# A decoder block on one core: both parts of each plain weight chunk written by transfers from GpSimd's queue

## The chip, the core and the metric

The kernel runs on one core of a Trainium2 chip. A core has five engines that run side by side, each through its own instruction queue in order: TensorE (PE in the profile) multiplies matrices into PSUM, VectorE (DVE) and ScalarE (ACT) work elementwise on SBUF and PSUM, GpSimd (POOL) works elementwise on SBUF, and SyncE (SP) only issues transfers. Transfers between device memory (HBM) and SBUF run on 16 DMA engines; SP, ACT and GpSimd can issue them. Engines wait for one another by semaphores.

The metric is the device time of one execution in microseconds, lower is better.

## The reference, cut to what matters

The block computes, for 512 tokens of width 1024 in float32, a token mixer with three branches, a cross-attention into 256 memory tokens, and a squared-ReLU MLP with 4096 hidden columns:

```python
h = rmsnorm(x, norm_mix_g[l])
proj = h @ w_in[l]
cb, cc, ch, sq, sk, sv, rq, rk, rv, rg, gate_logits = jnp.split(proj, SPLIT_POINTS, axis=-1)
conv_out = short_conv_mixer(cb, cc, ch, conv_w[l], conv_b[l])
sb_out = stick_breaking_attention(sq, sk, sv)
ret_out = retention(rq, rk, rv, rg, ret_norm_g[l])
branches = jnp.stack([conv_out, sb_out, ret_out], axis=2)
up = jnp.einsum('bsnw,nwd->bsnd', branches, w_branch[l])
gates = jax.nn.sigmoid(gate_logits.reshape(b, s, N_BRANCH, D_MODEL) + b_gate[l])
merged = jnp.sum(gates * up, axis=2)
x = x + merged @ w_o[l]
h = rmsnorm(x, norm_xa_g[l])
mem_n = rmsnorm(mem, norm_mem_g[l])
x = x + memory_attention(h, mem_n, w_xq[l], w_xkv[l], w_xo[l])
h = rmsnorm(x, norm_mlp_g[l])
x = x + squared_relu_mlp(h, w_up[l], w_down[l])
return rmsnorm(x, final_g)
```

Nearly all the work is in products of an activation of 512 tokens (256 for the memory) with a weight matrix.

## The kernel before

**Two parts.** TensorE multiplies float32r, a rounded float32. To keep float32 accuracy each operand is written as a sum of a high part, the value rounded to float32r, and a low part, the value minus the high part, rounded again. A product is three matmuls: high by high, high by low, low by high (`mm3`, lines 234 to 236). Activations are split when they are made (`split`, lines 223 and 224), weights when they have been loaded.

**Chunks.** Every weight matrix lies in HBM in chunks of 128 partitions by 1024 float32 columns, 512 KB. There are two kinds of entries:

- `Plain` is one chunk. Its raw values come into a `w_raw` tile, and `parts_of` makes the parts: ACT writes the high part `wh` (line 111), VectorE the low part `wl` (line 112).
- `Seven` is two chunks for a product that is put together from seven smaller ones (`seven`, line 290). It has four steps: two make parts of raw halves and chunks, two make parts of mixtures that VectorE computes first (`w_mix`). It is used for half of the gates and for three quarters of the up projection.

**Buffers.** `w_raw` has 3 buffers (RAWS), `w_part` 11 (WBUFS). A plain chunk takes two `w_part` buffers, a Seven entry seven.

**The stream.** `run_plan` goes through the items of the plan in order. `Stream.loads` lists all raw loads in the order of first use and `Stream.steps` all steps; each step notes how many loads it needs. Before an item's matmuls `pump` makes the steps up to two beyond those the item needs (AHEAD), and ahead of each step `load` issues raw loads, up to three from the entry's first one, on SP's queue (line 178). The order in which each engine finally gets its instructions is not this program order: a scheduler goes through the whole program ahead of time and gives each engine the earliest instruction in program order that its own timing model holds to be ready and that has a free buffer. That order is then fixed.

**The start.** `first_loads` issues on SP the first tile of x, the gain, two raw chunks, the second tile of x, one more chunk, and the last two tiles of x. The first product (`sv`, the values of the stick-breaking attention) runs token tile by token tile, so that each of its four token tiles needs the same four chunks.

**What GpSimd does.** Constants at the start; two masks in each of the 32 stick-breaking steps (`diag`, line 479), one in front of VectorE's scan and one in front of TensorE's transpose; one product per rotary half (line 612) and per retention head (line 675); the power of -1/2 in every norm (line 348), which VectorE waits for. It issues no transfers.

Of the kernel before, what the change touches and what calls it, by code (L numbers as in the profile page):

```python
# [10 lines left out]
F32 = mybir.dt.float32  # L11
F32R = mybir.dt.float32r
AF = mybir.ActivationFunctionType
ALU = mybir.AluOpType

P = 128
# [11 lines left out]
CW = 1024  # L28
# [5 lines left out]
RAWS, WBUFS, AHEAD = 3, 11, 2  # L34
# [4 lines left out]
def trunk_kernel(ctx: ExitStack, tc: tile.TileContext, x, mem, par, rot, dqd, kdec, g_mix, g_xa, g_mem, g_mlp,  # L39
                 g_fin, w_in, w_gate, w_br, w_o, w_xq, w_xk, w_xv, w_xo, w_up, w_up7, w_down, out):  # L40
    nc = tc.nc
    te, act, dve, pool = nc.tensor, nc.scalar, nc.vector, nc.gpsimd

    const = ctx.enter_context(tc.tile_pool(name="const", bufs=1))
    wpool = ctx.enter_context(tc.tile_pool(name="wpool", bufs=1))
# [6 lines left out]
    def unit(name, shape=(P, 2, 512), dt=F32R):  # L52
        return upool.tile(list(shape), dt, name=name, tag="u", bufs=UNITS)
# [10 lines left out]
    class Split:  # L64


        def __init__(self, name, n, cols=512):
            self.per = 1024 // cols
            self.n, self.cols = n, cols
            self.h = [unit(name + "_h", (P, self.per, cols)) for _ in range(n // self.per)]  # L70
            self.l = [unit(name + "_l", (P, self.per, cols)) for _ in range(n // self.per)]
# [19 lines left out]
    def load_g(g, eng=None):  # L91
        g_bc = unit("g_bc", (P, D), F32)
        (eng or act).dma_start(out=g_bc, in_=g.rearrange("(o d) -> o d", o=1).broadcast_to([P, D]))
        return g_bc
# [8 lines left out]
    def parts_of(src):  # L103
        n = src.shape[1]
        part = lambda: wpool.tile([P, CW], F32R, name="w_part", bufs=WBUFS)
        if 2 * n <= CW:
            both = part()
            wh, wl = both[:, :n], both[:, n:2 * n]
        else:
            wh, wl = part(), part()  # L110
        act.copy(out=wh, in_=src)  # L111
        dve.tensor_tensor(out=wl, in0=src, in1=wh.bitcast(F32), op=ALU.subtract)  # L112
        return wh, wl

    class Plain:


        def __init__(self, t, c):
            self.loads = [(t, c)]
            self.steps = [lambda raw: parts_of(raw[0])]  # L120
            self.parts = []

        def get(self):
            return self.parts[0]
# [35 lines left out]
    class Stream:  # L160
        def __init__(self, entries):
            self.loads = [l for e in entries for l in e.loads]
            self.steps, first = [], 0
            for e in entries:
                e.first = first
                for i, st in enumerate(e.steps):
                    self.steps.append((e, st, first + (len(e.loads) if i else 1)))
                first += len(e.loads)
                e.last = len(self.steps)
            self.raw = {}  # L170
            self.nd = self.ns = 0
# [222 lines left out]
    def first_loads():  # L394
        xs = S["xs"] = [unit("x", (P, D), F32) for _ in range(NT)]
        ld = lambda t: nc.sync.dma_start(out=xs[t], in_=x[t * P:(t + 1) * P, :])
        st = S["stream"]
        ld(0)
        S["g"] = load_g(g_mix, nc.sync)
        act.preload_act_table_set("natural_log_exp_and_others")  # L400
        st.load(2)
        ld(1)
        st.load(3)
        ld(2)
        ld(3)
        act.dma_start(out=prm, in_=par)
        act.dma_start(out=kdt, in_=kdec)
        S["hT"] = Split("hT", KT)
# [4 lines left out]

    hT = lambda: S["hT"]
    item(first_loads)
    item(lambda: norm_x0(0))
    item(lambda: norm_T(0, S["hT"], 0))
# [733 lines left out]
```

## Time and profile before

| | us |
|---|---|
| median of 2 runs | 1033.89 (1033.83 to 1033.95) |
| the profiled execution | 1033.71 |
| its span, from the first to the last instruction | 1032.0 |
| TensorE busy in it | 1015.5 |
| VectorE busy | 648.8 |
| ACT busy | 500.7 |
| GpSimd busy | 66.2 |

The profile is one execution. A busy share is an average over stages with different limits; a row of a view names the line of the kernel, the engine, the operation, the tile written and the tiles read, a count after an x, the busy time and the mean of one in nanoseconds, and then the time that the engine sat idle in front of it with what ended it. Issue instructions of the transfers stand under SPq, ACTq and POOLq and are not counted as busy.

### The profile page before, as it was taken

The page shows a single profiled execution, that of the slowest core. Times are in us where ns is not written, and L with a number is a line of the kernel's source. Part 1 is how long each engine was busy: PE and PEld are TensorE (multiplying, and loading weights), DVE is VectorE, ACT ScalarE, POOL GpSimd, SP SyncE. Part 2 cuts the span into 40 slices and gives each one's busy share as a digit, 9 for nine tenths or more (in the row PEclk, how much of TensorE's full clock was granted, in tenths as well). Part 3 has the DMA queues.
Part 4 walks back from the last instruction along what each step waited for, and adds up shares of the span by engine and source line. Part 5 has one row for each costly group of instructions (what it writes and reads, how often), then busy time and mean ns, then how long its engine had stood idle before and what let it go on. Part 6 is the DMA issues. An engine that isn't in the chain of part 4 may idle for free.

```text
span 1032.0 us, 14325 instructions
## 1 busy us (share of the span) xinstructions
PE 1015.5 (98%) x5636; PEld 884.9 (86%) x5636; DVE 648.8 (63%) x992; ACT 500.7 (49%) x887; POOL 66.2 (6%) x118
## 2 busy tenths in 40 slices
PE   6999999999999999999999999999999999999997
PEld 4888888888888889998898888898889989989985
DVE  5567777856563796784584555466947566565643
ACT  6465567766532154463463444345416624643741
POOL 1101112321110000000100000000000000000000
PEclk9999999999999999999999999999999999999999
DMA  6322233213122212335354213223222321332222
GB/s 265 103 102 81 83 104 102 82 42 123 62 87 79 100 62 83 103 119 198 133 184 163 82 47 118 81 83 123 86 79 82 125 92 71 124 123 80 103 85 81
DMA packets 29876, 106.33 MB, mean 103 GB/s; under 512 B 3569, under 2 KB 3569, under 8 KB 29809
## 3 DMA queue, kind: packets, MB, share of 16 engines
q1 hardware_dynamic: 27216, 98.05, 27.7%
q10 hardware_dynamic: 2592, 7.37, 2.0%
q8 instruction: 44, 0.72, 0.3%
q14 instruction: 24, 0.19, 0.1%
HBM read 103.31 MB, written 2.10 MB: 102 GB/s over the span
## 4 chain that ended last, share of the span: by engine, by line
PE 97%; DMA 1%; DVE 0%; ACT 0%; SPq 0%; issue 0%; DVEq 0%; POOLq 0%; POOL 0%
PE mm L235 24%; PE mm L234 24%; PE mm L236 24%; PE p L290 17%; PE at L385 1%; PE o L546 1%; PE aT L512 1%; DMA w_raw<-in_w_in_dram 1%; PE z L488 1%; PE z L489 0%; PE xsc L236 0%; PE xsc L235 0%; PE xsc L234 0%; PE ro L693 0%; PE sc L667 0%; PE xpp L929 0%
## 5 line engine op out<-in xcount | busy, mean ns | idle before, releaser
L112 DVE TENSOR_TENSOR w_part<-w_raw,w_part 128x1024 fp32r<-128x1024 f32 (+1 forms) x180 | 210.9, 1176 | 168.1 <-PE mm L235 75.2
L111 ACT CAST w_part<-w_raw 128x1024 fp32r<-128x1024 f32 (+1 forms) x180 | 180.6, 1006 | 135.2 <-PE mm L236 79.1
L234 PE MATMUL mm<-hT_h,w_part 128*128 128x512 f32 (+1 forms) x512 | 193.6, 379 | 0.0
L235 PE MATMUL mm<-hT_l,w_part 128*128 128x512 f32 (+1 forms) x512 | 193.3, 378 | 0.0
L236 PE MATMUL mm<-hT_h,w_part 128*128 128x512 f32 (+1 forms) x512 | 193.0, 378 | 0.0
L290 PE MATMUL p<-mix_h,w_part 128*128 128x256 f32 x576 | 112.2, 283 | 0.5 <-ACT sv_s L297 0.5
L236 PEld LDWEIGHTS mm<-hT_h,w_part 128*128 128x128 f32 x512 | 96.4, 188 | 17.1
L234 PEld LDWEIGHTS mm<-hT_h,w_part 128*128 128x128 f32 x512 | 96.2, 188 | 16.8
L235 PEld LDWEIGHTS mm<-hT_l,w_part 128*128 128x128 f32 x512 | 96.5, 188 | 16.4
L235 PE MATMUL mm<-w_part,u_h 128*128 128x512 f32 x256 | 99.8, 390 | 0.0
L234 PE MATMUL mm<-w_part,u_h 128*128 128x512 f32 x256 | 98.6, 390 | 0.0
L236 PE MATMUL mm<-w_part,u_l 128*128 128x512 f32 x256 | 98.2, 389 | 0.0
L290 PEld LDWEIGHTS p<-mix_h,w_part 128*128 128x128 f32 x576 | 93.4, 192 | 1.4 <-ACT sv_s L297 0.7
L290 PE MATMUL p<-hT_h,w_part 128*128 128x256 f32 x432 | 84.4, 283 | 0.0
L290 PE MATMUL p<-mix_l,w_part 128*128 128x256 f32 x288 | 81.5, 283 | 0.0
L290 PEld LDWEIGHTS p<-hT_h,w_part 128*128 128x128 f32 x432 | 70.1, 192 | 0.8
L111 ACT CAST w_part<-w_mix 128x1024 fp32r<-128x1024 f32 x36 | 37.8, 1051 | 55.9 <-PE mm L235 37.5
L112 DVE TENSOR_TENSOR w_part<-w_mix,w_part 128x1024 fp32r<-128x1024 f32 x36 | 44.0, 1221 | 26.7 <-ACT w_part L111 20.0
L290 PE MATMUL p<-hT_l,w_part 128*128 128x256 f32 x216 | 60.7, 283 | 0.0
L236 PEld LDWEIGHTS mm<-w_part,u_l 128*128 128x128 f32 x256 | 48.1, 188 | 9.8
L235 PEld LDWEIGHTS mm<-w_part,u_h 128*128 128x128 f32 x256 | 48.1, 188 | 9.5
L234 PEld LDWEIGHTS mm<-w_part,u_h 128*128 128x128 f32 x256 | 47.9, 188 | 9.5
(211 smaller groups left out, 1813.2 us busy)
## 6 DMA issues: line engine op xcount, KB each, us to landing
w_raw<-in_w_in_dram SPq DMA_DIRECT2D x52, 512.0 KB, 3.4
w_raw<-in_w_up_dram SPq DMA_DIRECT2D x32, 512.0 KB, 3.6
w_raw<-in_w_down_dram SPq DMA_DIRECT2D x32, 512.0 KB, 3.4
w_raw<-in_w_br_dram SPq DMA_DIRECT2D x12, 512.0 KB, 3.4
w_raw<-in_w_gate_dram SPq DMA_DIRECT2D x12, 512.0 KB, 3.5
w_raw<-in_w_o_dram SPq DMA_DIRECT2D x8, 512.0 KB, 3.5
w_raw<-in_w_xk_dram SPq DMA_DIRECT2D x8, 512.0 KB, 4.2
w_raw<-in_w_xv_dram SPq DMA_DIRECT2D x8, 512.0 KB, 3.5
```

The source lines that it names most:

```text
L111: act.copy(out=wh, in_=src)
L112: dve.tensor_tensor(out=wl, in0=src, in1=wh.bitcast(F32), op=ALU.subtract)
L234: te.matmul(ps, lh, rh, start=first, stop=False)
L235: te.matmul(ps, lh, rl, start=False, stop=False)
L236: te.matmul(ps, ll, rh, start=False, stop=last)
L290: te.matmul(ps[:, :256], x[:, k, :], y, start=first and k == 0 and i == 0, stop=k == 3 and i == 2, skip_group_check=True)
L385: te.transpose(ps[:, k * P:(k + 1) * P], xn[:, c * P:(c + 1) * P], ident)
L488: te.matmul(z[:, :s], q[:, e, tsl], S["skh", hp][:, e, :s], start=True, stop=False)
L512: te.transpose(aps[:, sb * P:(sb + 1) * P], a[:, sb * P:(sb + 1) * P], ident)
L546: te.matmul(dst, vv, rhs, start=sb == 0 and i == 0, stop=sb == nblk and i == 1, skip_group_check=True)
```

## The change

For a plain chunk the raw load, ACT's rounding and VectorE's subtraction are replaced. The step now takes two `w_part` tiles, has GpSimd issue a transfer from HBM straight into `wh` that rounds to float32r on the way, has ACT write the negative of `wh` into `wl`, and has GpSimd issue a second transfer from the same HBM chunk that adds to `wl` in place. A plain entry lists no raw loads any more, so only Seven entries use `w_raw` and SP's queue, and the stream counts the loads that a step needs accordingly. The two calls that loaded raw chunks between the first tiles of x are removed.

```diff
         def __init__(self, t, c):
-            self.loads = [(t, c)]
-            self.steps = [lambda raw: parts_of(raw[0])]
+            self.loads, self.src = [], (t, c)
+            self.steps = [self.step]
             self.parts = []
+
+        def step(self, raw):
+            t, c = self.src
+            wh, wl = [wpool.tile([P, CW], F32R, name="w_part", bufs=WBUFS) for _ in range(2)]
+            pool.dma_start(out=wh, in_=t[c])
+            act.activation(out=wl, in_=wh.bitcast(F32), func=AF.Copy, scale=-1.0)
+            pool.dma_start(out=wl, in_=t[c], accum_op=ALU.add)
+            return wh, wl
...
                 for i, st in enumerate(e.steps):
-                    self.steps.append((e, st, first + (len(e.loads) if i else 1)))
+                    self.steps.append((e, st, first + (len(e.loads) if i else min(1, len(e.loads)))))
...
         ld(0)
         S["g"] = load_g(g_mix, nc.sync)
         act.preload_act_table_set("natural_log_exp_and_others")
-        st.load(2)
         ld(1)
-        st.load(3)
         ld(2)
         ld(3)
```

## The prediction

> **What bounds the kernel now.** I read the page's first lines and its table of engines, then the chain of work that ended last, then the busy time of each engine in stretches of the span, and only then the waits.
>
> ```profile
> span 1032.0 us, 14325 instructions
> PE 1015.5 (98%) x5636; PEld 884.9 (86%) x5636; DVE 648.8 (63%) x992; ACT 500.7 (49%) x887; POOL 66.2 (6%) x118
> ...
> PE 97%; DMA 1%; DVE 0%; ACT 0%; SPq 0%; issue 0%; DVEq 0%; POOLq 0%; POOL 0%
> ...
> 0.00:26.00 26.00, 16.76 (x63) 12.62 (x64) 14.47 (x26) 15.51 (x33) 2.96 (x12) 1.00 0.69 263
> 26.00:1010.00 984.00, 983.49 (x5509) 860.01 (x5508) 625.95 (x951) 482.68 (x847) 61.07 (x103) 1.00 0.29 99
> 56.00:237.00 181.00, 181.00 (x880) 151.32 (x879) 131.24 (x197) 114.61 (x218) 37.72 (x71) 1.00 0.24 82
> 447.00:590.00 143.00, 143.00 (x835) 126.68 (x834) 87.69 (x133) 69.04 (x123) 3.32 (x6) 1.00 0.43 149
> 1010.00:1032.00 22.00, 15.21 (x68) 12.25 (x66) 8.37 (x15) 2.54 (x8) 2.20 (x4) 0.95 0.25 95
> ```
>
> A row with a colon gives a stretch, then the busy time of PE, weight loads, DVE, ACT and POOL, the granted clock, the DMA share and GB/s. From 26 to 1010 us TensorE is busy for 983.49 of 984 us at full clock, so there the change can only lose. TensorE is free for 9.2 us in the first stretch and for 6.8 us in the last. The matmuls are untouched: even with both ends gone the span would be 1015.5 us. Work taken from VectorE buys almost nothing.
>
> **The change part by part: what goes.**
>
> ```profile
> L112 DVE TENSOR_TENSOR w_part<-w_raw,w_part 128x1024 fp32r<-128x1024 f32 (+1 forms) x180 | 210.9, 1176 | 168.1 <-PE mm L235 75.2
> L111 ACT CAST w_part<-w_raw 128x1024 fp32r<-128x1024 f32 (+1 forms) x180 | 180.6, 1006 | 135.2 <-PE mm L236 79.1
> ...
> L111 ACT CAST w_part<-w_mix 128x1024 fp32r<-128x1024 f32 x36 | 37.8, 1051 | 55.9 <-PE mm L235 37.5
> ...
> q1 hardware_dynamic: 27216, 98.05, 27.7%
> q10 hardware_dynamic: 2592, 7.37, 2.0%
> ...
> SPq L178 <- DVE w_part L112: 783.5, 143, 21.2
> ...
> DMA to landing us min/median/max: 3.3/3.5/8.3
> ```
>
> A Seven entry makes two parts from mixtures and two from loads. 36 mixture parts are 18 Seven entries, which take 36 of the 180 parts made from loads; 144 are plain chunks. For these, 144 subtractions leave VectorE, 144 x 1.18 = 170 us, worth 0 by the paragraph above: TensorE covers them. ACT keeps one pass per chunk: the negation is a pass of the size of the cast, so I take the cast's 1.05 us (bounds: the row's mean 1.01 and the mixture row's 1.05). Nothing is won or lost there.
>
> **What DMA gains in work.** SP's queue moved 98.05 MB in 27.7% of 1032 us, 286 us of all 16 engines; a 0.524 MB chunk is 1.53 us. The rounding transfer takes the place of the raw load; I take 1.53 us for it, since it moves the same bytes. The adding transfer is new. Its lower bound is a copy, 1.53 us; it must also fetch its own destination, which doubles what is read, so the upper bound that I use is 3.06 us, and I take that end because the second read has no way round. 144 x 3.06 = 441 us of DMA more in the whole kernel, on some 310 us: 73% of the span, enough on average, but not everywhere.
>
> The Trainium skill ("Collectives: The Full Stack", section "The bandwidth ceiling: the fold count and why AG ≠ RS ≠ AR") says that a reducing transfer ran at half a copy's rate because of its two source reads and not because of the addition. By that the sum is the one at 3.06; by the bare row of the copy, 1.53, the K/V term below would be nothing. No run here shows an adding transfer yet.
>
> **What latency grows.** SP's loads sit in three raw buffers and wait for VectorE to empty them (783.5 us of SP's time, 143 times); ACT and VectorE in turn wait for TensorE to give a w_part buffer back. So today a freed buffer is refilled in 1.05 + 1.18 = 2.2 us. After, a freed buffer must first be written by the rounding transfer, and a second one by ACT and the adding transfer: issue, landing 3.5, ACT 1.05, issue, landing 3.5 + 1.53. GpSimd's issue price stands in no row. The nearest are SP's issue and GpSimd's own longest kind of pass:
>
> ```profile
> L178 SPq DMA_DIRECT2D w_raw<-in_w_xk_dram x8: 327/328/328, 486.6 to 522.9; - x8
> ...
> 208.78 1.30 POOL L612 TENSOR_TENSOR r_sw<-r_sw,rot 128x512 f32<-128x512 f32 x1
> ...
> 20.25 0.39 PE L234 MATMUL mm<-w_part,hT_h 128*128 128x512 f32 x1
> ...
> 25.71 0.39 PE L234 MATMUL mm<-w_part,hT_h 128*128 128x512 f32 x1
> ...
> 523.21 0.28 PE L234 MATMUL mm<-mT_h,w_part 128*128 128x256 f32 x1
> ...
> 523.57 0.28 PE L234 MATMUL mm<-mT_h,w_part 128*128 128x256 f32 x1
> ...
> 380.50 7.19 PE p L290 x60
> ```
>
> I take 1.3 us, the GpSimd row, since the same engine does it in software; 0.33 is the low end. 288 issues are then 374 us, with the 66 us there 43% of GpSimd. A refill is 1.3 + 3.5 + 1.05 + 1.3 + 5.0 = 12.2 us. What covers it: 24 matmuls of 512 columns are one plain chunk, 25.71 - 20.25 = 5.46 us. Eleven buffers hold the chunk in use and 4.5 chunks behind it, 4.5 x 5.46 = 24.6 us. Covered. With 256 columns (w_xk) three matmuls take 0.36 us, a chunk 2.9 us, the cover 13 us: just enough, if DMA keeps up. A w_br chunk behind a Seven can start when the Seven before it has ended, one chunk and 84 matmuls of 0.12 us earlier, 5.46 + 10.1 = 15.5 us: covered by 3 us. So w_down, up7 and the gates cost 0; if a refill took 18 us instead, the six w_br chunks behind a Seven would cost 2.5 us each.
>
> **The start.** Two early loads leave SP's queue, so x comes earlier; but all four chunks of the first projection are needed for its first tokens, and the fourth chunk's low part decides now:
>
> ```profile
> 19.68 0.19 PEld L235 LDWEIGHTS mm<-w_part,hT_h 128*128 128x128 f32 x1 [0.28 <-DVE w_part L112]
> ```
>
> Before that point DMA must then bring one x tile and the gain row (3.1 us), four rounding transfers (6.1) and four adding ones (6.1 to 12.2): 15.3 to 21.4 us, from about 2 us on, with about 2 us to land. Beside them go three more x tiles, three raw chunks for the first Sevens, which are now asked for at the first pump instead of much later, and a fifth and sixth rounding transfer, 12 us at most. The low part comes between 19 and 36 us: 0 to +16, I take the middle, +8.
>
> **The K/V stretch.** From 447 to 590 us there are 32 plain chunks (w_o, w_xk, w_xv, w_xq, eight each). DMA is busy for 0.43 x 143 = 61 us. With 32 x 3.06 = 98 us more it is 159 us, 16 over the stretch; with 1.53 it is 110 and fits. Chunks held ahead take some of it: 0 to +16, I take +8.
>
> **GpSimd's queue.** It runs in order, and it holds the two masks of each of the 32 stick-breaking steps and the norms' powers. An adding transfer waits at its head for ACT's negation, and ACT for the landing: whatever stands behind it waits too, at most 3.5 + 1.05 us, and two issues of 1.3. Who waits then: VectorE's scan, ACT's exponential and TensorE's transposes. Their slack now:
>
> ```profile
> 69.75 0.29 POOL L479 TENSOR_SCALAR_AFFINE_SELECT sb_suf<-sb_suf 128x128 f32<-128x128 f32 x1 [2.85 <-ACT sb_suf L503]
> ...
> 73.94 0.27 PE L512 MATMUL aT<-ident,sb_suf 128*128 128x128 f32 x1
> 74.77 0.29 POOL L479 TENSOR_SCALAR_AFFINE_SELECT sb_suf<-sb_suf 128x128 f32<-128x128 f32 x1 [3.12 <-ACT sb_suf L503]
> ...
> 79.21 0.27 PE L512 MATMUL aT<-ident,sb_suf 128*128 128x128 f32 x1
> ```
>
> The mask ends at 70.04 and 75.06, the transpose starts 3.9 and 4.2 us later: about 4 us of slack. Two issues (2.6 us) fit in; a full block (7.15 us) overruns by 3.1 us, in all steps 32 x 3.1 = 100 us. The order is chosen ahead of time by readiness, so a transfer that is not ready should stand behind the next chunk's first transfer and the masks; I take a quarter of a microsecond per step, +8, between 0 and 100. The norms' powers wait in the same way, ten within the loop, 0 to 4.6 us each against a token's matmuls of 5.46 us: +2, and 0 if they fit. The last four come after the last transfer: 0.
>
> **Sum.** The profiled execution took 1033.7 us, against a median of 1033.9. 1033.7 + 8 + 8 + 8 + 2 = 1060 us.
>
> **The rivals.**
> - *All hidden but the start.* The buffers cover the refill, the second read is cheaper than a whole one, and masks stand ahead of the transfers. For it: 24.6 against 12.2 us, and the 4 us of slack. Against: the 0.43 DMA share of the K/V stretch. It decides when the adding transfer costs under about 2.5 us of all engines: then 61 + 32 x 2.5 = 141 us fits into 143. Time 1033.7 + 6 = 1040 us, not slower by 2%.
> - *The queue blocks in every step.* If GpSimd's order puts an adding transfer straight after its own rounding one, a chunk occupies the queue for 1.3 + 3.5 + 1.05 + 1.3 = 7.15 us, more than the 5.46 us of its matmuls. 1033.7 + 8 + 8 + 100 = 1150 us. Against it: an order by readiness, and eleven buffers that let four rounding transfers go first.
> - *The adding transfer is the bound.* It decides when both transfers take over 5.46 us, an addition over 3.9. At four copies, 6.1 us, the chunks take 144 x 7.65 = 1101 us of DMA; what else there is, (27.7 + 2.0)% of 1032 less 144 x 1.53, is 86: 1190 us or more. No row speaks for or against it.
> - *Faster.* Over 2% would be under 1013 us, below TensorE's 1015.5 us. It would take fewer matmuls.
>
> **How the numbers follow.** About 2% either way, 1013 to 1055 us, is what a measurement of this kernel can tell from no change. Forecast (some of each term, 1050 to 1080): 0.46. All hidden but the start: 0.33. Blocked queue: 0.11. Slow addition: 0.08. Faster: 0.02. So slower by over 2%: 0.46 + 0.11 + 0.08 = 0.65; within 2%: 0.33; faster: 0.02. The range goes from 1038 (the hidden case with a good start) to 1180 (the blocked queue with the upper ends at the start and in the K/V stretch), which leaves out the slow addition, the gain and the best of the hidden cases, some 0.17. The forecast's own range is 1050 to 1080.
>
> **What would show it.** VectorE at about 480 us, ACT still at 500; SP's queue down to some 22 MB and a new queue with 151 MB; HBM reads up by 75 MB. The first stretch should show TensorE waiting for an adding transfer at about 28 us; the 447 to 590 stretch should lengthen by about 8 us at a DMA share above 0.9; 700 to 1010 should keep its length. GpSimd's issues should be near 1.3 us, landings 3.5 and 5. Wrong would be: TensorE waits for w_part in the w_down stages (refill over 24 us, or DMA full), masks that come over 4 us late in most steps (the blocked queue), or no wait at all after 30 us.

## The result and the profile after

The changed kernel takes 1118.78 us (median of 2 runs, 1117.74 to 1119.83) against 1033.89 us. The ratio is 1.0821, 95% interval 1.0790 to 1.0852: slower by 85 us, where the prediction had +26 and a range up to 1180.

The page of the changed kernel: its span, the engines, three lines on DMA and the chain of work that ended last.

```profile
span 1118.1 us, 14424 instructions
...
PE 1043.2 (93%) x5636; PEld 894.8 (80%) x5636; DVE 486.1 (43%) x848; ACT 499.6 (45%) x887; POOL 263.0 (24%) x406
...
q0 software_dynamic: 41472, 151.01, 59.5%
q1 hardware_dynamic: 6480, 22.55, 5.6%
...
HBM read 178.81 MB, written 2.10 MB: 162 GB/s over the span
...
issue 22%; PE 17%; POOL 7%; DMA 5%; ACT 1%; DVE 1%; POOLq 0%; DVEq 0%; ACTq 0%
```

The work is what was foreseen: VectorE at 486 us, ACT at 500, 151 MB on the new queue, 22.55 MB on SP's. GpSimd's 263 us hold its issues of transfers: unlike SP's and ACT's, they stand under the engine itself here and count as busy. What is new is TensorE. Its idle time rose from 1032.0 - 1015.5 = 16.5 us to 1118.1 - 1043.2 = 74.9 us, and for the same 5636 matmuls it was busy 27.7 us longer. The chain, once 97% TensorE, now runs mostly elsewhere (its shares add up to about half of the span; the rest the view doesn't place, so I use it for this one statement only).

Where the time was lost: first or last matmul that reads a tile, from the views of the tiles, in us. The row of `z` is the first step of stick-breaking, `rt_out` the last up projection of the retention branch, `mgs` the product with w_o, `xq_h` the first scores of the cross-attention, `xo_h` the product with w_xo, `u_h` w_down.

| | z first | rt_out last | mgs last | xq_h first | xo_h first | u_h first | u_h last | span |
|---|---|---|---|---|---|---|---|---|
| before | 55.2 | 471.6 | 519.3 | 572.8 | 637.1 | 728.9 | 1024.4 | 1032.0 |
| after | 71.3 | 499.4 | 557.7 | 626.0 | 702.6 | 795.3 | 1108.0 | 1118.1 |
| later by | 16.1 | 27.8 | 38.4 | 53.2 | 65.5 | 66.4 | 83.6 | 86.1 |

The busy times of after in such stretches (PE, weight loads, DVE, ACT, POOL, clock, DMA share, GB/s):

```profile
0.00:56.00 56.00, 34.56 (x132) 26.94 (x133) 17.41 (x38) 19.93 (x46) 13.78 (x26) 0.94 0.67 190
60.00:270.00 210.00, 208.81 (x1010) 173.25 (x1009) 107.28 (x182) 129.69 (x242) 82.84 (x147) 1.00 0.79 174
499.40:626.00 126.60, 105.12 (x545) 87.10 (x544) 31.81 (x63) 43.41 (x82) 35.75 (x52) 0.95 0.88 221
...
795.30:1090.00 294.70, 282.47 (x1699) 250.87 (x1698) 140.28 (x206) 136.98 (x228) 40.07 (x56) 1.00 0.56 142
```

So there are three large places: the start (16.1 us), w_o to the cross-attention (rt_out last to xo_h first, 65.5 - 27.8 = 37.7 us, at a DMA share of 0.88 in its first part), and w_down (83.6 - 66.4 = 17.2 us, at a DMA share of only 0.56, a mean that is taken apart below). A smaller one, 27.8 - 16.1 = 11.7 us, lies between the first step of stick-breaking and the end of the up projections. The stick-breaking stretch, where the prediction feared GpSimd's queue, is not one: TensorE is busy 208.81 of 210 us (and waits another 2.05 us at 274.79, just behind the row).

Who waited for whom: TensorE's waits, then the longest of the other engines (sum, times, longest, in us).

```profile
PE at L393 <- DVE xn L384: 19.3, 3, 8.6
PE mm L243 <- DMA w_part<-in_w_down_dram: 7.0, 5, 2.8
PE mm L243 <- DMA w_part<-in_w_xv_dram: 5.9, 3, 2.8
PE mm L244 <- DMA w_part<-in_w_xk_dram: 5.4, 6, 1.6
```

```profile
POOL w_part L128 <- ACT w_part L127: 244.9, 103, 6.0
POOL w_part L126 <- PE mm L244: 172.0, 38, 22.9
POOL w_part L126 <- PE p L298: 161.8, 8, 52.4
...
ACT w_part L127 <- DMA w_part<-in_w_down_dram: 61.3, 22, 5.2
```

L126 is the rounding transfer, L127 the negation, L128 the adding transfer. The largest row is an adding transfer at the head of GpSimd's queue, held 103 times for ACT's negation, and ACT itself waits for the rounding to land (209 us in 77 places over all matrices). Roundings wait as well, 334 us in 46 places, for TensorE to give a buffer back; none of these waits falls between 566 and 642 us, the stretch shown next. The time from issue to landing, of line 126 and then of line 128:

```profile
DMA to landing us min/median/max: 3.6/6.3/11.9
```

```profile
DMA to landing us min/median/max: 5.2/6.9/12.3
```

The prediction had 3.5 and 5.0: these are the minima, not the medians. Last, GpSimd's own order in the stretch of w_xk, w_xv and w_xq (start, duration, line, idle time before it with its releaser):

```profile
566.04 0.88 POOL L128 DMA_DIRECT2D w_part<-in_w_xk_dram  x1 [2.78 <-ACT hT_h L231]
...
588.46 0.87 POOL L128 DMA_DIRECT2D w_part<-in_w_xv_dram  x1 [2.94 <-ACT w_part L127]
589.01 0.88 POOL L126 DMA_DIRECT2D w_part<-in_w_xv_dram  x1
592.52 0.87 POOL L128 DMA_DIRECT2D w_part<-in_w_xv_dram  x1 [2.63 <-ACT w_part L127]
593.07 0.88 POOL L126 DMA_DIRECT2D w_part<-in_w_xv_dram  x1
598.84 0.86 POOL L128 DMA_DIRECT2D w_part<-in_w_xv_dram  x1 [4.89 <-ACT w_part L127]
...
642.04 0.87 POOL L128 DMA_DIRECT2D w_part<-in_w_xq_dram  x1 [3.27 <-ACT w_part L127]
```

From 566 to 642 us the queue alternates strictly, adding, rounding, adding, rounding, and it always waits at the adding. Each adding belongs to the rounding before the last: the rounding of 589.01 gets its adding at 598.84, 9.8 us later, and in these 9.8 us two chunks go out. From 566.04 to 642.04 there are 16 intervals, 76.0 / 16 = 4.75 us per chunk. TensorE uses up a chunk of w_xk or w_xv in 2.9 us. The instruction list of GpSimd has this order nearly throughout: at 134 of the 144 addings exactly one further rounding stands in front, at the other 10 none.

### The profile page after: what moved, and what is told of

Its sections match the earlier page's. It is cut to its first block, busy times and chain, and to the rows that moved or that the text cites. A ratio compares the mean times of both kernels' runs of the same rounds, so it can differ in the third digit from the quotient of the medians.

```text
span 1118.1 us, 14424 instructions
## 1 busy us (share of the span) xinstructions
PE 1043.2 (93%) x5636; PEld 894.8 (80%) x5636; DVE 486.1 (43%) x848; ACT 499.6 (45%) x887; POOL 263.0 (24%) x406
## 3 DMA queue, kind: packets, MB, share of 16 engines
q0 software_dynamic: 41472, 151.01, 59.5%
q1 hardware_dynamic: 6480, 22.55, 5.6%
## 4 chain that ended last, share of the span: by engine, by line
issue 22%; PE 17%; POOL 7%; DMA 5%; ACT 1%; DVE 1%; POOLq 0%; DVEq 0%; ACTq 0%
PE p L298 5%; PE mm L243 4%; PE mm L244 4%; PE mm L242 4%; POOL w_part L126 4%; DMA w_part<-in_w_down_dram 3%; POOL w_part L128 3%; DMA w_part<-in_w_o_dram 2%; DMA w_part<-in_w_xo_dram 1%; ACT w_part L127 0%; DMA w_part<-in_w_up_dram 0%; DVE w_part L112 0%; DVE x L842 0%; PE at L393 0%; ACT w_part L111 0%
## 5 line engine op out<-in xcount | busy, mean ns | idle before, releaser
L127 ACT ACTIVATE w_part<-w_part 128x1024 fp32r<-128x1024 f32 x144 | 152.5, 1059 | 298.9 <-DMA w_part<-in_w_down_dram 61.3
L842 DVE TENSOR_TENSOR x<-mm,x 128x512 f32<-128x512 f32 x48 | 32.4, 688 | 72.4 <-PE mm L244 72.4
L126 POOL DMA_DIRECT2D w_part<-in_w_down_dram x32 | 25.4, 795 | 157.0 <-PE p L298 155.7
L128 POOL DMA_DIRECT2D w_part<-in_w_in_dram x52 | 45.7, 878 | 59.2 <-ACT w_part L127 38.0
```

The source lines that it names most:

```text
L126: pool.dma_start(out=wh, in_=t[c])
L127: act.activation(out=wl, in_=wh.bitcast(F32), func=AF.Copy, scale=-1.0)
L128: pool.dma_start(out=wl, in_=t[c], accum_op=ALU.add)
L842: dve.tensor_tensor(out=dst, in0=ps, in1=dst, op=ALU.add)
```

## The experiments

**What a transfer costs by itself.** Nothing but transfers of 512 KB chunks: eight of each kind in a row, then one of each alone. The kernel leaves the whole block out.

```diff
+        ("pool_round", F32R, lambda t, s: pool.dma_start(out=t, in_=s)),
+        ("pool_add", F32, lambda t, s: pool.dma_start(out=t, in_=s, accum_op=ALU.add)),
```

> Only transfers of 512 KB chunks, in groups of eight: loads from SP, plain loads from GpSimd, rounding ones, adding ones without and with rounding; then one of each alone. Theory A (the second read of the adding transfer is the price): eight loads and eight rounding ones take 12 to 14 us of all engines, eight adding ones 24 to 26; alone an adding one lands 1.5 us after a rounding one. Theory B (the transfers are cheap, the fixed order of the queues is the price): all groups take 12 to 14 us, and an adding one alone lands in under 4 us.

Median us to landing, of eight and of one:

```profile
sp_copy<-in_w_in_dram SPq DMA_DIRECT2D x8, 512.0 KB, 7.1
...
pool_round<-in_w_in_dram POOLq DMA_DIRECT2D x8, 512.0 KB, 7.1
pool_add<-in_w_in_dram POOLq DMA_DIRECT2D x8, 512.0 KB, 11.7
...
pool_round_one<-in_w_in_dram POOLq DMA_DIRECT2D x1, 512.0 KB, 3.7
pool_add_one<-in_w_in_dram POOLq DMA_DIRECT2D x1, 512.0 KB, 5.1
```

Its timeline shows the pace of a full queue, since VectorE reads one value of each chunk as soon as it lands:

```profile
50.34 0.15 DVE L59 COPY tok<-pool_round 128x1 f32<-128x1 f32 x1 [1.12 <-DMA pool_round<-in_w_in_dram]
51.61 0.15 DVE L59 COPY tok<-pool_round 128x1 f32<-128x1 f32 x1 [1.12 <-DMA pool_round<-in_w_in_dram]
...
74.26 0.15 DVE L59 COPY tok<-pool_add 128x1 f32<-128x1 f32 x1 [2.35 <-DMA pool_add<-in_w_in_dram]
76.77 0.15 DVE L59 COPY tok<-pool_add 128x1 f32<-128x1 f32 x1 [2.35 <-DMA pool_add<-in_w_in_dram]
```

A rounding transfer lands every 51.61 - 50.34 = 1.27 us, as a copy from SP does (1.28); an adding one every 76.77 - 74.26 = 2.51 us. Rounding is free, adding costs twice a copy, and the upper end that the prediction took was right in kind. That the fetch of the destination is what doubles the time, and not the addition, no run here separates; "the second read" below stands for both. Alone they land after 3.7 and 5.1 us, as predicted. The Trainium skill's sentence that the prediction cited ("Collectives: The Full Stack", section "The bandwidth ceiling: the fold count and why AG ≠ RS ≠ AR"), half a copy's rate for a reducing transfer, agrees with this run. Both transfers of a chunk together need 3.78 us of a full queue, more than the 2.9 us of a chunk of 256 columns.

**The second read taken away.** The second transfer overwrites instead of adding, so the low part is the chunk rounded once more and not the remainder; the order of GpSimd's queue stays the same.

```diff
-            pool.dma_start(out=wl, in_=t[c], accum_op=ALU.add)
+            pool.dma_start(out=wl, in_=t[c])
```

> The adding transfer is replaced by a second rounding one, so the low part holds the high part; order of all queues and every wait as in the changed kernel. Theory A (DMA work and landing time of the adding transfer): at least half of the 85 us comes back, 1075 us or less, the K/V stretch and the w_down rounds nearly as before. Theory B (GpSimd's and ACT's queues wait in order for the rounding transfer's landing): the waits are all still there, 1100 us or more.

1057.30 us (1055.79 to 1058.64), ratio 1.0227 (1.0211 to 1.0242): 61.5 of the 85 us are gone.

```profile
q0 software_dynamic: 41472, 151.01, 44.1%
```

The same bytes take 44.1% of 1054.1 us instead of 59.5% of 1118.1 us, 200 us less, 1.4 us per adding. A rounding transfer now lands after 4.6 us (median) instead of 6.3.

**The negation on VectorE instead of ACT.**

```diff
-            act.activation(out=wl, in_=wh.bitcast(F32), func=AF.Copy, scale=-1.0)
+            dve.tensor_scalar(out=wl, in0=wh.bitcast(F32), scalar1=-1.0, scalar2=None, op0=ALU.mult)
```

> VectorE writes the negative instead of ACT. Theory B with ACT as the blocked queue (210 us of ACT waiting for rounding transfers, norms and splits behind it): 20 us or more come back, under 1100 us. Theory A: ACT's wait only fills time in which DMA is late anyway, within 10 us of 1119.

1123.89 us, ratio 1.0873 (1.0855 to 1.0891): no gain. The wait for the landing costs no less in VectorE's queue than in ACT's; what it costs in either, this run does not tell. In the changed kernel's own timeline it shows twice: the sums of squares of the third token tile stand in ACT's queue behind negations that waited 6.39 and 2.77 us for landings, and start at 37.73 us instead of 22.28, and TensorE's wait of 2.05 us at 274.79 is for an exponential of stick-breaking behind a negation that waited 4.88 us.

**One stage the old way.** For the named chunks the raw load, ACT's rounding and VectorE's subtraction are put back: the four chunks of the first product; those of w_o, w_xk, w_xv and w_xq; those of w_down.

```diff
+            if 'w_in' in t.tensor.name and 20 <= c < 24:
+                self.loads = [(t, c)]
+                self.steps = [lambda raw: parts_of(raw[0])]
```

> Only the four chunks of the first projection are made the old way (load on SP, ACT rounds, VectorE subtracts). If the loss of 23 us at the start comes from these chunks' chain of transfers, 15 to 23 us come back: 1096 to 1104. If it comes from what stands behind in GpSimd's queue (norm powers behind later chunks' transfers), less than 10 come back.

> The 32 chunks of w_o, w_xk, w_xv and w_xq are made the old way, all others by transfers. If the K/V stretch loses its 37 us to its own transfers (DMA work of rounding and adding there), 30 us or more come back: 1080 to 1090. If the delay is only carried in from earlier (late norms, late start), less than 15 come back.

> The 32 chunks of w_down are made the old way. Refill theory (after a Seven entry only four buffers are left, and a refill of some 16 us is longer than the 11 us of cover): the 17 us of the four rounds come back, 1098 to 1104. If the rounds are late because of DMA work carried over from before, less than 8 come back.

| old way for | us | ratio (interval) | less than after |
|---|---|---|---|
| first product | 1114.50 | 1.0766 (1.0743 to 1.0789) | 4 |
| w_o, w_xk, w_xv, w_xq | 1081.71 | 1.0462 (1.0443 to 1.0481) | 37 |
| w_down | 1099.91 | 1.0634 (1.0586 to 1.0682) | 19 |

The last two agree with the table of places. The first does not: with it `z` begins at 63.4 us, 8 earlier than after, but `xo_h` at 701.2, only 1.4 earlier. What was won at the start was lost again where the parts run short.

**One half of the change alone.** First the adding half: SP loads raw, ACT rounds and negates, GpSimd only adds. The transfers' work stays the same. Then the rounding half: GpSimd rounds, SP loads raw too, VectorE subtracts.

```diff
-            pool.dma_start(out=wh, in_=t[c])
+            act.copy(out=wh, in_=raw[0])
```

> SP loads the raw chunk ahead as before, ACT rounds it into the high part and writes its negative, GpSimd's transfer adds: the same DMA work as in the changed kernel (a copy and an addition per chunk), but the first half of the chain is hidden behind the raw buffers. DMA-work theory: little changes, 1095 to 1120. Chain theory (issue, landing, negation, issue, landing in a row): at least 30 us come back, under 1090.

```diff
-            act.activation(out=wl, in_=wh.bitcast(F32), func=AF.Copy, scale=-1.0)
-            pool.dma_start(out=wl, in_=t[c], accum_op=ALU.add)
+            dve.tensor_tensor(out=wl, in0=raw[0], in1=wh.bitcast(F32), op=ALU.subtract)
```

> GpSimd's transfer rounds into the high part, SP loads the raw chunk, VectorE subtracts: two copies per chunk in DMA and no addition. DMA-work theory: as with the copy in place of the addition or better, 1040 to 1058. Chain theory: the same wait for a landing from GpSimd's queue stands in front of VectorE, 1060 or more.

The adding half takes 1083.67 us, ratio 1.0481 (1.0466 to 1.0497): with the same bytes and the same 144 addings 35 us are gone, so the DMA engines' throughput alone is not the cause. The rounding half takes 1044.99 us, ratio 1.0110 (1.0095 to 1.0125); its `z` begins at 64.0 us, 8.8 late, and that is nearly all of its 11 us.

**More and fewer buffers.** My theory at this point was the prediction's own picture with larger numbers: a refill of 0.87 + 6.3 + 1.06 + 0.87 + 6.9 = 16 us against what the buffers hold.

```diff
-UNITS, SCRS = 30, 9
-RAWS, WBUFS, AHEAD = 3, 11, 2
+UNITS, SCRS = 28, 9
+RAWS, WBUFS, AHEAD = 3, 13, 2
```

> The changed kernel with 13 w_part buffers instead of 11 (and two activation buffers fewer, to make room). Theory A (a freed buffer's refill, 0.87 + 6.3 + 1.06 + 0.87 + 6.9 = 16 us at the median, outlasts what the other buffers hold): one chunk more ahead gives 5.5 us more cover at 512 columns and 2.9 at 256, so at least 20 us come back, 1099 us or less, with the K/V and w_down stages shorter. Theory B (the DMA engines' throughput alone): the same bytes and the same doubled reads in the same stretches, within 8 us of 1118.8.

> The kernel before with the same 13 w_part buffers and two activation buffers fewer: the control for the run with 13 buffers. Both theories: its refill is 2.2 us, covered by far, and TensorE is busy without a gap, so within 3 us of 1033.7. If the activation buffers matter, it is slower, and that difference is to be taken off the other.

With 9 buffers UNITS stays at 30.

> The changed kernel with 9 w_part buffers, all else the same. Theory A: 3.5 chunks held behind the one in use cover 19 us at 512 columns and 10 at 256, against a refill of 16 at the median and up to 25: at least 30 us more than the change, 1149 us or over. Theory B (DMA throughput): within 8 us of 1118.8.

> The kernel before with 9 w_part buffers, the control: both theories, within 5 us of 1033.7, since 2.2 us of refill are covered by 3.5 chunks as well as by 4.5.

| w_part buffers | after | before |
|---|---|---|
| 9 | 1120.87, ratio 1.0840 (1.0809 to 1.0871) | 1033.98, 1.0002 (0.9993 to 1.0011) |
| 11 | 1118.78, ratio 1.0821 (1.0790 to 1.0852) | 1033.76 |
| 13 | 1125.85, ratio 1.0887 (1.0855 to 1.0919) | 1036.72, 1.0031 (1.0019 to 1.0042) |

The theory fell: neither 20 us won nor 30 lost. But DMA throughput, its rival, had already fallen by the adding half alone. A third is needed, and the order of GpSimd's queue gave it: with 13 buffers as well, exactly one rounding stands in front of 134 addings. More buffers cannot be used by an order that never asks for them.

**Three roundings ahead.** A chunk's step first issues the roundings of the next two plain chunks. `round` issues a chunk's rounding if it hasn't been issued. At 123 of the 144 addings (121 with 13 buffers) three roundings now stand in front. The second kernel has the overwriting transfer (its low part is not the remainder), the third 13 buffers.

```diff
+            for _ in range(3):
+                if isinstance(e, Plain):
+                    e.round()
+                    e = e.next
```

> The changed kernel, but a chunk's step first issues the roundings of the next two plain chunks (unless a Seven entry stands between), so that GpSimd's queue holds three roundings ahead of each adding transfer instead of one; same transfers, same buffers, same engines. Theory C (the in-order queue with one rounding ahead sets a period of half a rounding's landing, negation and issues, 4.6 us per chunk in the K/V stretch): the period falls to what the DMA engines allow, 3.8 us (1.27 + 2.5), the K/V stretch gives back some 15 of its 37 us and w_down most of its 19: 1075 to 1095 us. Theory B (the DMA engines' throughput): within 8 us of 1118.8.

> The same three roundings ahead, with a plain transfer in place of the adding one (the low part is then the raw chunk, not the remainder). Theory C with the DMA engines as the second bound: without the second read a chunk takes 2.5 us of DMA, less than the 2.9 of the K/V stretch, and with the deeper queue nothing is left but the start: 1040 to 1050 us, 10 us or so below the 1057 of the copy with one rounding ahead. If the queue is not it: 1057 again.

> The three roundings ahead with 13 w_part buffers (two activation buffers fewer, worth +3 us in the kernel before). Theory C: if the buffers bind once the order allows them, 5 us or more below the run with 11; if the DMA engines bind by then, within 5 us of it.

| | us | ratio (interval) |
|---|---|---|
| three ahead, 11 buffers | 1110.48 | 1.0735 (1.0712 to 1.0759) |
| three ahead, 11 buffers, overwriting | 1058.83 | 1.0252 (1.0228 to 1.0275) |
| three ahead, 13 buffers | 1084.05 | 1.0494 (1.0477 to 1.0510) |

The order alone gives 8 us and misses its expectation; the buffers alone gave nothing; both together give 35. The waits with 11 buffers say why (L128 is the rounding here, L139 the adding):

```profile
POOL w_part L128 <- PE mm L257: 307.1, 75, 23.0
...
POOL w_part L139 <- ACT w_part L138: 99.4, 85, 6.0
```

Addings wait 99 us instead of 245, but the roundings in front of them now wait 307 us for TensorE to free a buffer, and hold up the addings behind. With 13 buffers the queue runs like this at w_xq:

```profile
583.10 0.88 POOL L139 DMA_DIRECT2D w_part<-in_w_xq_dram  x1 [2.01 <-ACT w_part L138]
...
586.78 0.88 POOL L139 DMA_DIRECT2D w_part<-in_w_xq_dram  x1 [2.25 <-ACT w_part L138]
...
594.30 0.87 POOL L139 DMA_DIRECT2D w_part<-in_w_xq_dram  x1 [2.29 <-ACT w_part L138]
```

594.30 - 583.10 is three intervals, 3.73 us per chunk: the 1.27 + 2.51 us of the transfers measured by themselves. Here the DMA engines are the bound: from 560 to 600 us they move 282 GB/s at a share of 1.09 (the share adds up the packets' times and can pass 1). The changed kernel had 222 GB/s at a share of 0.95 from 566 to 642 us, so a share near 1 was not yet the ceiling there. Without the second read, three ahead is worth nothing (1058.83 against 1057.30 with one ahead), which misses too. As far as these runs show, one rounding ahead is too few only while the adding transfers make the roundings land late.

**What is left.** All three have three roundings ahead and 13 buffers. The first moves the power of -1/2 of the norms of one token tile to ACT; the second has the first four chunks and the first loads as before; the third has this start and overwrites instead of adding.

```diff
-        pool.tensor_tensor(out=r, in0=ms, in1=half[:, :n], op=ALU.pow)
+        if n == 1:
+            act.activation(out=r, in_=ms, func=AF.Ln)
+            act.activation(out=r, in_=r, func=AF.Exp, scale=-0.5)
```

> Three roundings ahead, 13 buffers, and the power of -1/2 of the norms of one token tile made by ACT (a logarithm and an exponential on 128 values) instead of GpSimd. If the start is late because the powers stand behind adding transfers in GpSimd's queue: the first stick-breaking step 8 us or more earlier than without, and 1076 us or less. If it is late because the first chunks' low parts land late: within 4 us of 1084.

> Three roundings ahead, 13 buffers, and the four chunks of the first product made the old way, with the two early raw loads put back between the tiles of x. Theory (the start's delay is the four chunks on GpSimd's queue, and it was given back later only because the supply of parts bound there): the first stick-breaking step some 12 us earlier than without, and most of it kept to the end: 1068 to 1075 us. If it is given back again: 1080 or more.

> As the run with three roundings ahead, 13 buffers and the old start, with a plain transfer in place of the adding one (the low part is then the raw chunk, not the remainder). Theory (start, queue order, buffers and the second read are all there is): as the kernel before with 13 buffers, 1036.7, to within 5 us. If something else costs time (GpSimd's issues in front of the masks, the powers, the clock), 1045 or more.

The powers on ACT take 1096.25 us, ratio 1.0608 (1.0589 to 1.0627), 12 more than without, and `z` begins at 73.2 us instead of 70.9: neither expectation. They brought in table loads, 13 on each of the two new lines:

```profile
L370 ACT ACT_TABLE_LOAD x13 | 16.7, 1283 | 0.2
L371 ACT ACT_TABLE_LOAD x13 | 16.7, 1283 | 0.2
```

That is 33 us more on the engine that makes the negations. The changed kernel's own timeline answers the question that this run does not: each of its 22 powers starts at most 0.72 us after the value that it reads is made, so none stood behind a transfer for long.

With the old start the kernel takes 1071.72 us, ratio 1.0369 (1.0352 to 1.0385), as expected: `z` begins 13.8 us earlier (57.1 against 70.9), and 12.3 us remain at the end. With the supply of parts loosened, a gain at the start is kept.

The last takes 1040.67 us, ratio 1.0066 (1.0051 to 1.0082), 4 us above the kernel before with 13 buffers. Its page, then GpSimd's queue at w_xq (L131 is the rounding):

```profile
span 1038.6 us, 14440 instructions
...
PE 1018.4 (98%) x5636; PEld 884.4 (85%) x5636; DVE 489.0 (47%) x852; ACT 500.5 (48%) x887; POOL 206.7 (20%) x398
```

```profile
542.03 0.53 POOL L131 DMA_DIRECT2D w_part<-in_w_xq_dram  x1 [1.33 <-PE mm L260]
...
544.91 0.53 POOL L131 DMA_DIRECT2D w_part<-in_w_xq_dram  x1 [1.33 <-PE mm L260]
```

One chunk every 544.91 - 542.03 = 2.88 us, and the queue waits for TensorE: the supply is ahead again. The whole loss is now laid out, in this order of removal: order and buffers 1118.78 to 1084.05, 34.7 us; the start, to 1071.72, 12.3; the second read, to 1040.67, 31.1; a rest of 4.0 to the kernel before with 13 buffers, and the 3.0 that this kernel itself takes more than with 11. Unrounded that is 85.0, the difference to 1033.76. The sizes hang on the order of removal: the second read taken away first is worth 61.5, and then the queue's order is worth nothing. The lengths of the stages, from the views of the tiles, show which step repaired which:

| us | before | after | three ahead, 13 buffers | and old start | and overwriting |
|---|---|---|---|---|---|
| to z first | 55.2 | 71.3 | 70.9 | 57.1 | 57.2 |
| z first to rt_out last | 416.4 | 428.1 | 417.5 | 420.7 | 416.3 |
| rt_out last to xo_h first | 165.5 | 203.2 | 183.1 | 184.7 | 165.3 |
| xo_h first to u_h first | 91.8 | 92.7 | 92.5 | 92.4 | 91.9 |
| u_h first to last | 295.5 | 312.7 | 308.1 | 307.2 | 298.3 |

Order and buffers repair the second row and half of the third; the second read is the other half of the third, and the larger part of w_down's. Two other runs agree on w_down: 295.4 us with its chunks made the old way, and 297.6 with the overwriting transfer and one rounding ahead.

Why w_down feels the transfers at a DMA share of 0.56 is told in part by the changed kernel's timeline. That share is a mean of rounds of eight chunks of w_down and of the Seven products between the rounds (columns as above):

```profile
872.00:911.00 39.00, 35.88 (x195) 30.63 (x193) 8.72 (x16) 18.29 (x29) 11.30 (x16) 1.00 0.89 216
911.00:960.00 49.00, 48.78 (x333) 45.41 (x334) 33.09 (x47) 22.89 (x39) 0.00 (x0) 1.00 0.28 87
```

```profile
871.95 0.55 POOL L126 DMA_DIRECT2D w_part<-in_w_down_dram  x1 [52.43 <-PE p L298]
...
882.90 0.49 PE L243 MATMUL mm<-w_part,u_h 128*128 128x512 f32 x1 [1.58 <-DMA w_part<-in_w_down_dram]
```

The first rounding of the round waits 52 us for a buffer that a Seven product still reads, and the low part of its chunk is there 11 us later, 1.58 us after TensorE ran out of work. All eight chunks are then made in one burst. The next two rounds go the same way (waits of 49.9 us, shares of 0.90).

No version here beats the kernel before; the nearest that computes the block is the rounding half alone, 1045.0 us.

## Why the prediction was right and wrong

Right: slower, because an idle TensorE cannot be made up; VectorE's 170 us worth nothing; the bytes; ACT unchanged; twice a copy's work for an adding transfer; GpSimd's issues below the 1.3 us taken (0.6 to 0.9). That 1119 us lies inside the stated range is luck: its upper part stood for masks held up in the stick-breaking steps, where TensorE waited 3 us in all.

Wrong, by its own steps:

- *"Eleven buffers hold the chunk in use and 4.5 chunks behind it, 4.5 x 5.46 = 24.6 us. Covered."* This is the step that failed, with *"an order by readiness, and eleven buffers that let four rounding transfers go first"*. The order lets one go first, and the number of buffers has no say as long as it does (9, 11 and 13: 1121, 1119, 1126 us). The cover was counted in buffers; the pace is set by the queue, two chunks in 9.8 us. The cost of 0 for w_down and the gates followed from it; the old way is worth 19 us at w_down, though order and buffers give back only 4.6 of that, and the second read more. There the cover was also counted from too early: the Seven products hold the buffers, so the first rounding of a round goes out at 871.95, only 9.4 us before TensorE runs out of work at 881.3, and not 24.6.
- *"landing 3.5 ... landing 3.5 + 1.53"*. Right for a transfer alone (3.7 and 5.1), but among the others the medians are 6.3 and 6.9. By these medians and the issues of 0.87 us the refill comes to some 16 us, not 12.2. The prediction had a DMA share of 73% and worked out landings as on an idle queue.
- *K/V, +8 (0 to +16).* The mechanism named, transfers that outrun the DMA engines, is there (0.88 DMA share, 3.73 us per chunk where the order doesn't bind), but the term was mis-sized: the old way is worth 37 us. It lacked the queue's own pace, 4.75 us per chunk against 2.9, and it averaged 2.9 and 5.46 us chunks over 143 us, so that the ones at 5.46 seemed to pay for the others.
- *The start, +8 (0 to +16).* `z` is 16.1 us late, the upper end; with the supply loosened it is worth 12.3. TensorE waited for the last of the first four low parts until 35.1 us, where the prediction had about 28. Other waits there, 5.24 and 3.67 us, ended with VectorE's passes of the norms. How the 16.1 us divide between the two stays open.
- *GpSimd's queue in the stick-breaking steps, +8 (0 to +100).* About 3: TensorE's transposes of these steps waited 3.2 us in three places. The queue did block as the second rival had it, but the masks had slack and the parts had none later.
- *The norms' powers, +2.* About 0: 0.72 us of delay at most, as shown above.
- *In no term:* TensorE busy 27.7 us longer.
- Two of its sums are slightly off, and nothing hangs on them: the late end of the start, 2 + 21.4 + 12.2 + 2, is 37.6 and not 36 us, and the blocked queue with both upper ends and the powers is 1168, not 1180 us.

The rival that all is hidden but the start fell; its condition, an adding transfer under about 2.5 us, was nearly met (2.51 by itself), but it looked at throughput alone. The slow addition, from 3.9 us on, fell by the price measured.

## What to carry to other kernels

When work moves to transfers on one in-order queue, write down the order of that queue: a transfer that waits for an engine lets out only what stands in front of it, and buffers beyond that are never used. The supply rate is the number of chunks in flight over issue, landing under load and the engine's pass between, and it is to be held against the demand of the fastest stage, not of the mean one. Depth in the order and buffers have to be raised together, and an adding transfer to be counted as two.

## What the runs showed of the hardware

In several places TensorE ran slower for some 3 us soon after a short wait. In the changed kernel's timeline, matmuls of 512 columns around a wait of 2.03 us:

```profile
26.50 0.50 PE L243 MATMUL mm<-w_part,hT_h 128*128 128x512 f32 x1 [2.03 <-DMA w_part<-in_w_in_dram]
...
28.39 0.63 PE L242 MATMUL mm<-w_part,hT_h 128*128 128x512 f32 x1
28.81 0.63 PE L243 MATMUL mm<-w_part,hT_h 128*128 128x512 f32 x1
...
31.45 0.40 PE L242 MATMUL mm<-w_part,hT_h 128*128 128x512 f32 x1
31.68 0.40 PE L243 MATMUL mm<-w_part,hT_h 128*128 128x512 f32 x1
```

and the busy times of that stretch:

```profile
26.80:30.10 3.30, 3.30 (x10) 2.50 (x9) 0.00 (x0) 1.06 (x1) 0.45 (x1) 0.53 1.04 212
```

At a granted clock of 0.53 they follow one another in 0.42 us, and from 30.5 us on in 0.23 again. The Trainium skill ("TensorE: Matmul & The Clock Gate", section "Part 1: The HAM clock gate (the "warmup" mystery)") gives half the clock after an idle window of about 3.4 us, and full clock after about as long a busy one. The half and the way back agree with these rows; the wait was shorter here, 2.03 us. TensorE had then been at the full pace for only about 1 us. But the wait of 2.26 us at 431.86, in front of which it had worked without a wait since 276 us, was followed by the same: from 433.5 to 436.5 us 512 columns took 0.42 to 0.43 us. After waits of 1.28 us (1059.32) and 1.58 us (882.90) the pace stayed at 0.23. Over the runs the busy time grows with the idle time: against the kernel before, 27.7 us more busy with 58.4 more idle (after), 13.6 with 26.0 (three ahead, 13 buffers, old start), 2.9 with 3.7 (the same, overwriting). That the one causes the other I have not tried; if it does, each us of waiting cost another half to three quarters of a us here.

An issue of an adding transfer lasts 0.87 us on GpSimd, against 0.53 for the one that overwrites, though the next issue starts 0.55 us behind it (588.46 and 589.01). The transfers of a loaded queue land later than alone: a rounding after 6.3 against 3.7 us, an adding one after 6.9 against 5.1.
